# One shared inverse square root for two head norms, and an output projection whose first token block runs two outputs ahead of its second

## The chip, the core and the metric

The kernel runs on one NeuronCore of a Trainium2 chip. Five engines work side by side, each through its own queue in order: TensorE (PE, with its weight loads PEld), VectorE (DVE), ScalarE (ACT), GpSimd (POOL) and SyncE (SP, which only issues transfers). They meet at semaphores. The metric is device time in microseconds (us) of one execution; lower is better.

## The reference, cut to what matters

One layer of a recurrent decoder runs over 1104 token columns: 16 meta tokens, 8 sequences of 8 sample tokens and 1024 prompt tokens. Between two feed-forward halves stands the mixing part, and the change lies only there:

```python
z = h @ lp['w_in']
u_r, g_r, u_m, z_m, q_g, k_g, v_g, g_g, a_lr = jnp.split(z, _split_points(), axis=-1)
...
y_m = jax.nn.sigmoid(z_m) * (head_rmsnorm(hm, lp['ml_norm_g']) + lp['ml_skip'] * cm)   # mLSTM mixer, h = num / denom
y_g = head_rmsnorm(og, lp['gla_norm_g']) * jax.nn.silu(g_g)                            # GLA mixer
y = jnp.concatenate([y_r, y_m, y_g], axis=-1) @ lp['w_out']
...
def head_rmsnorm(h, g):                       # 4 heads of 96
    y = h * lax.rsqrt(jnp.mean(h * h, axis=-1, keepdims=True) + EPS)
    return y.reshape(Bsz, L, H * Dh) * g
```

Both mixers are recurrent over chunks of tokens: a chunk needs the state that the chunk before it left.

## The kernel before

**Stages.** The program does the first feed-forward half, the mixing part (`mix`, some 840 to 1345 us in the profile), the rest of `w_out` together with the start of the second feed-forward half, and that half. Every big product is three products of fp32r pieces (high by high, low by high, high by low), and a weight tile is split by ACT (`whi`) and DVE (`wlo`), both in the helper `split`, L115 and L116.

**Blocks and chunks.** The tokens stand in three blocks of 336, 384 and 384 columns, and in nine chunks of 128 (chunk 0 has 80, with the sample tokens), three to a block. In `mix`, PE does the input projections (`unit`, tile `pw`, line L210 of the helper `gemm3`), which write z to DRAM, and beside them both mixers chunk by chunk. `m1`, `m2`, `m3` are the mLSTM of a chunk (scores; state and outputs `num`; head norm, gate and the split into `ys`), `g1`, `g2`, `g3` the same of the GLA (output `o_`). `msamp` and `gsamp` do the sample sequences of chunk 0. The loop over `c` writes m1 and g1 of chunk c, then `fin` (m3 and g3) of chunk c-1, then m2 and g2 of chunk c. `fin` of chunk 0 comes at c = 4, since its samples come late. In `ylru`, the third mixer's output of a block is split into `ys[b]`.

**What sets the order.** The program isn't run in the order of the code. A list scheduler orders it before the run, with its own idea of durations: everything in `tc.high_priority` (the mixers) goes first where it is ready, and the projections and `w_out` fill in. The engines then run that fixed order.

**Buffers that matter here.** A tag of a pool has so many slots, and a new tile of it waits until one is free. `T4`/`TT` share the tag `t` (4 slots), `G4`/`GT` the tag `tg` (3 slots), `zg` (the gate inputs of m3 and of g3) has a single slot, and the split weights have 7. `ys[0]` takes the slot of the operands of block 0, so `ylru(0)` holds two `tg` tiles until the last input projection of block 0 has read them:

```python
if j == 1:
    ys[b] = slot(b)
if j == 2:
    ylru(b)
```

**The norm.** m3 and g3 each square (ACT), sum by head (DVE) and call `rsq` (L119 to L127): 2 integer instructions and 3 Newton steps of 3, all on DVE and each waiting for the one before, on tiles of 128 partitions by 4 heads. m3 also folds its denominator `dn` in. Then ACT scales the four heads, PE transposes (`to_f`, tile `pyT`, L982), and DVE and ACT finish `y` and split it into `ys`.

**w_out.** At c = 7 the products of blocks 0 and 1 with `w_out` are written (tile `pwo`): eight outputs d of 24 matmuls for each block, from two PSUM banks. Those of block 2 follow in `wout2` (L1662), after the broadcast of the next norm (`rbp`, L259).

Of the kernel before, what the change touches and what calls it, by code (L numbers as in the profile page):

```python
# [10 lines left out]
AF = mybir.ActivationFunctionType  # L11
OP = mybir.AluOpType
AX = mybir.AxisListType
# [6 lines left out]
EPS = 1e-6  # L20
# [29 lines left out]
def tile_step(ctx, tc, A, O):  # L50
    nc = tc.nc
    V, S, G, PE = nc.vector, nc.scalar, nc.gpsimd, nc.tensor
# [12 lines left out]
    def pa(name):  # L65
        return psum["a"].tile([128, 512], F32, tag="a", name=name)
# [37 lines left out]
    slots, ys = {}, {}  # L104
# [9 lines left out]
    def split(hi, lo, x):  # L114
        S.copy(hi, x)  # L115
        V.tensor_tensor(lo, x, hi.bitcast(F32), OP.subtract)  # L116

    def rsq(tp, v, p, n, tag=""):
        y = tp.tile([128, 8], F32, tag="rsy" + tag, name="rsy", bufs=RB)[:p, :n]  # L119
        a = tp.tile([128, 8], F32, tag="rsa" + tag, name="rsa", bufs=RB)[:p, :n]  # L120
        V.tensor_scalar(a.bitcast(I32), v.bitcast(I32), 1, None, OP.arith_shift_right)
        V.tensor_scalar(y.bitcast(I32), a.bitcast(I32), -1.0, float(0x5F3759DF), OP.mult, OP.add)
        for _ in range(3):
            V.tensor_tensor(a, y, y, OP.mult)
            V.scalar_tensor_tensor(a, a, -0.5, v, OP.mult, OP.mult)
            V.scalar_tensor_tensor(y, a, 1.5, y, OP.add, OP.mult)
        return y  # L127
# [56 lines left out]
    def wraw(pool):  # L184
        return pool.tile([128, 4, 256], F32, tag="raw", name="wraw", bufs=2)

    def wpair(pool):
        return [pool.tile([128, 4, 128], F32R, tag=tag, name=tag, bufs=7) for tag in ("whi", "wlo")]

    def wload(*parts):  # L190
        raw = wraw(P["wp"]).rearrange("p k f -> p (k f)").rearrange("p (k f) -> p k f", f=128)
        for c, w, src in parts:
            if src is None:
                G.memset(raw[:, :, c : c + w], 0.0)
            else:
                nc.sync.dma_start(raw[:, :, c : c + w], src)
        u = []
        for c in range(2):
            u.append(wpair(P["wp"]))
            split(*u[c], raw[:, 4 * c : 4 * c + 4, :])  # L200
        return [h for h, _ in u], [l for _, l in u]
# [4 lines left out]
    def gemm3(p, w, x, ks, wsl, xsl):  # L206
        i, tot = 0, 3 * len(ks)
        for ww, xx in ((w[0], x[0]), (w[0], x[1]), (w[1], x[0])):
            for k in ks:
                PE.matmul(p, wsl(ww, k), xsl(xx, k), start=i == 0, stop=i == tot - 1)  # L210
                i += 1
# [300 lines left out]

    wo = A["w_out"].rearrange("(k p) f -> p k f", p=128)

    def w_out(bs, out):
        for d in range(8):
            u = wload((0, 128, wo[:, :, d * 128 : d * 128 + 128]))
            for b in bs:
                n, t0 = NB[b], 16 if b == 0 else 0
                p = pa("pwo")  # L520
                gemm3(p[:, t0:n], u, ys[b], range(8), wblock, lambda x, k: x[:, k, t0:n])
                out(b, d, p[:, t0:n])


# [12 lines left out]
    def mix(  # L537
# [73 lines left out]
        mt = ph.enter_context(tc.tile_pool(name="mt", bufs=2, reuse_waits="tile"))  # L611

        def U(shape, tag, bufs=None, dt=F32):
            pool = me if tag in ("um", "gr", "cm", "sm", "vx", "num0", "o0", "qf0", "vt0", "qe0", "klT0", "vx0") else mt
            return pool.tile(shape, dt, tag=tag, name=tag, bufs=bufs)

        def TT(p=128, n=384):
            return U([128, 388], "t", 4)[:p, :n]

        def T4(e=96):  # L620
            return U([128, 388], "t", 4)[:, : 4 * e].rearrange("p (h e) -> p h e", h=4)

        def GT(p=128, n=384):
            return U([128, 388], "tg", 3)[:p, :n]

        def G4(e=96):
            return U([128, 388], "tg", 3)[:, : 4 * e].rearrange("p (h e) -> p h e", h=4)
# [311 lines left out]
            nc.scalar.dma_start(O["s_n"], nt)  # L939


        def m3(b, j, x):
            cm, o, m, num, et = x[:5]
            dn = U([128, 4], "dn")[:m]
            V.scalar_tensor_tensor(dn, num[:m, :, 96], -1.0, num[:m, :, 96], OP.mult, OP.max)
            V.tensor_tensor(dn, dn, et[:m, 32:36], OP.max)
            V.reciprocal(dn, dn)
            sq = T4()
            S.activation(sq[:m], num[:m, :, 0:96], AF.Square)
            ss = U([128, 4], "ssm")[:m]  # L950
            V.tensor_reduce(ss, sq[:m], AX.X, OP.add)
            V.tensor_tensor(ss, ss, dn, OP.mult)
            V.scalar_tensor_tensor(ss, ss, 1.0 / 96.0, dn, OP.mult, OP.mult)
            V.tensor_scalar(ss, ss, EPS, None, OP.add)
            rr = rsq(mt, ss, m, 4, "m")
            V.tensor_tensor(rr, rr, dn, OP.mult)
            hn = sq
            for h in range(4):
                S.mul(hn[:m, h, :], num[:m, h, 0:96], rr[:, h : h + 1])
            z = U([128, 3, 128], "zg", 1)  # L960
            nc.sync.dma_start(z[:, :, :m], zd["z"][:, :, OFF[b] + o : OFF[b] + o + m])
            y = TT().rearrange("p (k t) -> p k t", k=3)
            for k in range(3):
                S.mul(y[:, k, :m], cm[:, k, :m], skh[:, k : k + 1])
            p = to_f(pn2, hn, m)
            for k in range(3):
                V.scalar_tensor_tensor(y[:, k, :m], p[:, k, :m], ngh[:, k : k + 1], y[:, k, :m], OP.mult, OP.add)
            V.scalar_tensor_tensor(y[:, :, :m], z[:, :, :m], 1.0, y[:, :, :m], OP.add, OP.mult)
            split(ys[b][0][:, 2:5, o : o + m], ys[b][1][:, 2:5, o : o + m], y[:, :, :m])
            if b == 2 and j == 2:  # L970
                nc.sync.dma_start(O["p_C"].rearrange("h d e -> d h e"), c1[:, :, 0:96])
                pn = pn2("pn")
                PE.transpose(pn[:4, 0:96], c1[:, :, 96], ident[:96, :96])
                nt = U([32, 128], "cst")
                S.copy(nt[:4, :96], pn[:4, 0:96])
                nc.scalar.dma_start(O["p_n"], nt[:4, :96])

        def to_f(pool, src, m):
            p = pool("pyT").rearrange("p (k t) -> p k t", k=4)
            s = src.rearrange("p h e -> p (h e)")  # L980
            for k in range(3):
                PE.transpose(p[:, k, :m], s[:m, k * 128 : k * 128 + 128], ident[:m, :m])  # L982
            return p
# [264 lines left out]
                    nc.sync.dma_start(O["s_S"][:, 2 * a + i].rearrange("s k v -> k s v"), ssm[64 * i : 64 * i + 48])  # L1248


        def g3(b, j, x):
            to, m, o_ = x[:3]
            sq = G4()
            S.activation(sq[:m], o_[:m], AF.Square)
            ss = U([128, 4], "ssg")[:m]
            V.tensor_reduce(ss, sq[:m], AX.X, OP.add)
            V.tensor_scalar(ss, ss, 1.0 / 96.0, EPS, OP.mult, OP.add)
            rr = rsq(mt, ss, m, 4, "g")
            on = sq
            for h in range(4):  # L1260
                S.mul(on[:m, h, :], o_[:m, h, :], rr[:, h : h + 1])
            g = U([128, 3, 128], "zg", 1)
            nc.sync.dma_start(g[:, :, :m], zd["g"][:, :, to : to + m])
            p = to_f(pg2, on, m)
            y = GT().rearrange("p (k t) -> p k t", k=3)
            V.tensor_tensor(y[:, :, :m], g[:, :, :m], p[:, 0:3, :m], OP.mult)
            o = to - OFF[b]
            split(ys[b][0][:, 5:8, o : o + m], ys[b][1][:, 5:8, o : o + m], y[:, :, :m])
            if b == 2 and j == 2:
                for a in range(2):  # L1270
                    for i in range(2):
                        nc.sync.dma_start(O["p_S"][2 * a + i], s1[64 * i : 64 * i + 48, a, i, :])
# [32 lines left out]
        el8 = U([128, 2, 8], "el8", 1)  # L1305

        def fin(x):
            m3(*x[0])
            g3(*x[1])

        x, x0 = None, None
        preps = {
# [2 lines left out]
        for c in range(9):  # L1315
            with tc.high_priority(offset=BOOST):
                b, j = divmod(c, 3)
                for f, i in preps.get(c, ()):
                    f(i)
                xm, xg = m1(b, j), g1(b, j)  # L1320
# [11 lines left out]
                x = (b, j, m2(b, j, xm)), (b, j, g2(b, j, xg))  # L1332
                if c == 0:
                    x0, x = x, None
# [4 lines left out]
        with tc.high_priority(offset=BOOST):  # L1339
            fin(x)  # L1340
# [138 lines left out]
    with ExitStack() as ph:  # L1479
# [84 lines left out]
        c0, n = THIRDS1[0][1], THIRDS1[0][0]  # L1564
# [25 lines left out]
        for b, (n, c0) in enumerate(THIRDS1):  # L1590
            x = xq.tile([128, 8, 384], F32, tag="xo", name="xo", bufs=2)[:, :, :n]
# [29 lines left out]
    with ExitStack() as ph:  # L1621
# [94 lines left out]
        for j, (n, c0, chunks, s0) in enumerate(THIRDS2):  # L1716
            x = tp.tile([128, 8, 384], F32, tag="xo", name="xo", bufs=2)[:, :, :n]
# [9 lines left out]
            ss = tp.tile([128, 3, 3], F32, tag="ssf", name="ssf", bufs=2)  # L1727
# [14 lines left out]
            for i, (o, m) in enumerate(chunks):  # L1742
                dst = O["y_sample"] if s0 + o < 0 else O["y_prompt"][s0 + o : s0 + o + 128, :]
                for q in range(2):
                    h = slice(q * 512, q * 512 + 512)
# [60 lines left out]
```

## Time and profile before

| what | value |
|---|---|
| three runs | 2164.37, 2165.81, 2166.42 us; median 2165.81 us |
| the profiled execution | 2165.65 us, of which the span of the page is 2163.9 us |
| PE busy | 2089.4 us, 97% of the span |
| DVE busy | 1299.5 us, 60% |
| ACT busy | 914.1 us, 42% |

Shares are averages over stages with different limits, so a change of one stage is read in that stage. A busy PE is not PE at its peak, since matmuls overlap: two that follow each other start closer together than one lasts. A product of plain fp32 operands stands twice in the trace and once in the program's order.

### The profile page before, as it was taken

The numbers are of one execution on the slowest core, as the hardware profiler recorded it, in microseconds if no ns is written. First come the engines' busy times: TensorE is split into PE (matmuls) and PEld (weight loads), VectorE is DVE, ScalarE is ACT, GpSimd is POOL, SyncE is SP. The second block draws the span as 40 slices with busy tenths as digits, with TensorE's granted clock in tenths as the row PEclk, the third lists the DMA queues.
The fourth block names the chain that finished last, engine by engine and source line by source line (L and its number), as shares of the span: only waits on it lengthen the run. The fifth ranks groups of instructions, "written<-read, shape, count | busy, mean of one in ns | idle before, by whom it ended". The sixth has DMA issues, their size and how long they took to land.

```text
span 2163.9 us, 38185 instructions
## 1 busy us (share of the span) xinstructions
PE 2089.4 (97%) x14600; PEld 2040.0 (94%) x14600; DVE 1299.5 (60%) x2861; ACT 914.1 (42%) x1965; POOL 270.7 (13%) x284
## 2 busy tenths in 40 slices
PE   6999999999999999999999899999999999999997
PEld 6999999999989999978997789999999999998997
DVE  7765555663565545866777786776555566356342
ACT  5433232342443434635655673443233234254332
POOL 0222232211100011000000000022323221000000
PEclk8999999999999999999999899999999999999999
DMA  6322222235574544444434245522322224667342
GB/s 213 105 83 95 90 71 70 82 126 167 187 245 138 200 138 116 131 139 129 114 87 111 75 119 156 190 69 82 99 83 81 70 81 133 201 222 244 127 142 83
DMA packets 292555, 275.50 MB, mean 127 GB/s; under 512 B 46751, under 2 KB 277188, under 8 KB 291860
## 3 DMA queue, kind: packets, MB, share of 16 engines
q1 hardware_dynamic: 287580, 271.27, 40.0%
q10 hardware_dynamic: 4792, 1.78, 0.4%
q8 instruction: 115, 1.88, 0.4%
q14 instruction: 68, 0.56, 0.1%
HBM read 212.99 MB, written 60.01 MB: 126 GB/s over the span
## 4 chain that ended last, share of the span: by engine, by line
PE 86%; DVE 5%; DMA 4%; ACT 3%; issue 1%; SPq 0%; POOL 0%; DVEq 0%; ACTq 0%; POOLq 0%
PE p L503 22%; PE b L365 15%; PE c L365 10%; PE a L365 10%; PE pw L210 9%; PE a L411 4%; PE b L411 4%; PE pwo L210 3%; DMA wraw<-in_ffn_w_dram 1%; PE pq L837 1%; PE pA L1039 1%; PE pwo L1662 1%; DVE wlo L116 1%; DMA hr<-hidden 1%; DMA bcc<-z_bc 0%
## 5 line engine op out<-in xcount | busy, mean ns | idle before, releaser
L116 DVE TENSOR_TENSOR wlo<-wraw,whi 128x512 fp32r<-128x512 f32 x508 | 360.7, 728 | 338.9 <-ACT whi L115 228.9
L115 ACT CAST whi<-wraw 128x512 fp32r<-128x512 f32 x508 | 302.7, 618 | 576.8 <-PE p L503 157.0
L503 PE MATMUL p<-h,whi 128*128 128x384 f32 (+2 forms) x2080 | 402.2, 331 | 0.7 <-ACT whi L115 0.6
L503 PEld LDWEIGHTS p<-h,whi 128*128 128x128 f32 x2080 | 354.9, 189 | 1.7 <-ACT whi L115 1.4
L365 PE MATMUL b<-op,whi 128*128 128x256 f32 (+2 forms) x1728 | 255.9, 289 | 0.4 <-DVE c L372 0.4
L365 PEld LDWEIGHTS b<-op,whi 128*128 128x128 f32 x1728 | 233.6, 189 | 0.7 <-DVE c L372 0.7
L503 PE MATMUL p<-h,wlo 128*128 128x384 f32 (+2 forms) x1040 | 222.3, 331 | 0.0
L372 DVE TENSOR_TENSOR c<-p,b 128x256 f32<-128x256 f32 (+2 forms) x216 | 94.6, 439 | 175.1 <-PE b L365 162.1
L342 POOL TENSOR_TENSOR ws<-wraw 128x512 f32<-128x512 f32 x72 | 105.2, 1461 | 728.0 <-DMA wraw<-in_ffn_w_dram 473.4
L503 PEld LDWEIGHTS p<-h,wlo 128*128 128x128 f32 x1040 | 181.0, 190 | 0.0
L365 PE MATMUL c<-op,whi 128*128 128x256 f32 (+2 forms) x1152 | 172.8, 289 | 0.3 <-DVE op L116 0.3
L365 PE MATMUL a<-op,whi 128*128 128x256 f32 (+2 forms) x1152 | 172.5, 289 | 0.0
L365 PEld LDWEIGHTS c<-op,whi 128*128 128x128 f32 x1152 | 155.7, 189 | 0.5 <-DVE op L116 0.5
L365 PEld LDWEIGHTS a<-op,whi 128*128 128x128 f32 x1152 | 155.1, 189 | 0.0
L365 PE MATMUL b<-op,wlo 128*128 128x256 f32 (+2 forms) x864 | 144.4, 289 | 0.0
L115 ACT CAST whi<-ws 128x512 fp32r<-128x512 f32 x144 | 88.4, 618 | 132.4 <-PE b L365 79.4
L365 PEld LDWEIGHTS b<-op,wlo 128*128 128x128 f32 x864 | 122.6, 189 | 0.0
L116 DVE TENSOR_TENSOR wlo<-ws,whi 128x512 fp32r<-128x512 f32 x144 | 100.2, 696 | 2.2 <-PE b L411 1.7
L210 PE MATMUL pw<-sh,whi 128*128 128x384 f32 (+1 forms) x480 | 97.3, 339 | 1.6 <-DVE stg L581 1.6
L372 DVE TENSOR_TENSOR c<-c 128x256 f32<-128x256 f32 (+2 forms) x144 | 62.8, 436 | 59.2 <-PE c L365 58.9
L210 PE MATMUL pw<-sh,wlo 128*128 128x384 f32 (+1 forms) x480 | 98.0, 339 | 0.0
L365 PE MATMUL a<-op,wlo 128*128 128x256 f32 (+2 forms) x576 | 96.4, 289 | 0.5 <-DVE wlo L116 0.5
(466 smaller groups left out, 3382.0 us busy)
## 6 DMA issues: line engine op xcount, KB each, us to landing
wraw<-in_ffn_w_dram SPq DMA_DIRECT2D x224, 512.0 KB
hr<-hidden SPq DMA_DIRECT2D x88, 192.0 KB
hidden<-h SPq DMA_DIRECT2D x36, 256.0 KB
wraw<-in_w_in_dram SPq DMA_DIRECT2D x16, 512.0 KB
wraw<-in_w_out_dram SPq DMA_DIRECT2D x16, 512.0 KB
wraw<-in_ffn_w_dram SPq DMA_DIRECT2D x24, 256.0 KB
hidden<-h SPq DMA_DIRECT2D x18, 296.0 KB
hidden<-h SPq DMA_DIRECT2D x18, 288.0 KB
```

The source lines that it names most:

```text
L115: S.copy(hi, x)
L116: V.tensor_tensor(lo, x, hi.bitcast(F32), OP.subtract)
L210: PE.matmul(p, wsl(ww, k), xsl(xx, k), start=i == 0, stop=i == tot - 1)
L342: G.tensor_tensor(t, x, y, op)
L365: PE.matmul(t[:, :n], ww[:, k, :], xx[:, k, :], start=first and i == 0, stop=i == 11, skip_group_check=True,)
L372: V.tensor_tensor(out, x, t[:, :n], OP.add)
L411: PE.matmul(p, w[:, k, :], x[:, k, :], start=c == 0, stop=c == 23)
L503: PE.matmul(ps_[e], t[k // 2][a][:, k % 2, e * 128 : e * 128 + 128], hs[k0 + k][b], start=k0 == 0 and i == 0, stop=k0 + nk == NFB and i == ...
L837: PE.matmul(p[:96, h, :m], wt[:, kb, sl, 0:96], cm[:, kb, :m], start=i == 0, stop=i == len(ks) - 1)
L1039: PE.matmul(p[:, a], x[:, a], y[:, a], start=True, stop=True)
L1662: PE.matmul(p, u[k // 4][a][:, k % 4, :], ys[2][b][:, k, :], start=i == 0, stop=i == 23)
```

## The change

`m3` and `g3` no longer have an `rsq` each: a new `norm` squares and sums both mixers' heads into one tile of 8 columns and calls `rsq` once. `w_out` writes block 0's output d, and block 1's output d - 2 behind it, so that up to three outputs' weights are held.

```diff
     def w_out(bs, out):
-        for d in range(8):
-            u = wload((0, 128, wo[:, :, d * 128 : d * 128 + 128]))
-            for b in bs:
+        u = {}
+        for i in range(10):
+            for b, d in ((bs[0], i), (bs[1], i - 2)):
+                if not 0 <= d < 8:
+                    continue
+                if d not in u:
+                    u[d] = wload((0, 128, wo[:, :, d * 128 : d * 128 + 128]))
                 n, t0 = NB[b], 16 if b == 0 else 0
                 p = pa("pwo")
-                gemm3(p[:, t0:n], u, ys[b], range(8), wblock, lambda x, k: x[:, k, t0:n])
+                gemm3(p[:, t0:n], u[d], ys[b], range(8), wblock, lambda x, k: x[:, k, t0:n])
                 out(b, d, p[:, t0:n])
...
-        def m3(b, j, x):
-            cm, o, m, num, et = x[:5]
+        def norm(xm, xg):
+            m, num, et, o_ = xm[2], xm[3], xm[4], xg[2]
             dn = U([128, 4], "dn")[:m]
...
-            sq = T4()
-            S.activation(sq[:m], num[:m, :, 0:96], AF.Square)
-            ss = U([128, 4], "ssm")[:m]
-            V.tensor_reduce(ss, sq[:m], AX.X, OP.add)
-            V.tensor_tensor(ss, ss, dn, OP.mult)
-            V.scalar_tensor_tensor(ss, ss, 1.0 / 96.0, dn, OP.mult, OP.mult)
-            V.tensor_scalar(ss, ss, EPS, None, OP.add)
-            rr = rsq(mt, ss, m, 4, "m")
-            V.tensor_tensor(rr, rr, dn, OP.mult)
-            hn = sq
+            ss = U([128, 8], "ssm")[:m]
+            sm, sg_ = T4(), G4()
+            for i, (sq, x) in enumerate(((sm, num[:m, :, 0:96]), (sg_, o_[:m]))):
+                S.activation(sq[:m], x, AF.Square)
+                V.tensor_reduce(ss[:, 4 * i : 4 * i + 4], sq[:m], AX.X, OP.add)
+            for _ in range(2):
+                V.tensor_tensor(ss[:, 0:4], ss[:, 0:4], dn, OP.mult)
+            V.tensor_scalar(ss, ss, 1.0 / 96.0, EPS, OP.mult, OP.add)
+            rr = rsq(mt, ss, m, 8, "m")
+            V.tensor_tensor(rr[:, 0:4], rr[:, 0:4], dn, OP.mult)
+            return rr, sm, sg_
...
-        def g3(b, j, x):
+        def g3(b, j, x, rr, on):
             to, m, o_ = x[:3]
-            sq = G4()
-            S.activation(sq[:m], o_[:m], AF.Square)
-            ss = U([128, 4], "ssg")[:m]
-            V.tensor_reduce(ss, sq[:m], AX.X, OP.add)
-            V.tensor_scalar(ss, ss, 1.0 / 96.0, EPS, OP.mult, OP.add)
-            rr = rsq(mt, ss, m, 4, "g")
-            on = sq
             for h in range(4):
-                S.mul(on[:m, h, :], o_[:m, h, :], rr[:, h : h + 1])
+                S.mul(on[:m, h, :], o_[:m, h, :], rr[:, 4 + h : 5 + h])
...
         def fin(x):
-            m3(*x[0])
-            g3(*x[1])
+            rr, sm, sg_ = norm(x[0][2], x[1][2])
+            m3(*x[0], rr, sm)
+            g3(*x[1], rr, sg_)
```

**What moves on PE at the first chunk's norm.** In PE's queue of before, in the middle of the input projections (`pw`), stand the transposes of chunk 1's mLSTM output (`pyT<-ident,t`), and soon after them chunk 2's state product (`pI<-c_9306,qf`):

```order
L1021 MATMUL pv<-ident,vf 128x128 x3
L921 MATMUL pI<-sm,qx 80x97 x2
L982 MATMUL pyT<-ident,t 128x128 x3
L210 MATMUL pw<-sh_7291,whi 128x384 x2
...
L1039 MATMUL pA<-qbd_9301,qk 32x2 x2
L875 MATMUL pI<-c_9306,qf 128x97 x4
L210 MATMUL pw<-sh_8865,whi 128x384 x8
```

In PE's queue of the change the same transposes and the same state product (lines L992 and L880 there) stand behind the last input projection:

```order
L210 MATMUL pw<-sh_8865,wlo 128x384 x8
L210 MATMUL pwo<-sh_11897,whi 128x320 x2
L1179 MATMUL pkl<-ident,h 128x128 x2
L1242 MATMUL pO<-sm,qx 80x96 x8
L992 MATMUL pyT<-ident,tg 128x128 x3
L210 MATMUL pwo<-sh_11897,whi 128x320 x2
L992 MATMUL pyT<-ident,t 128x128 x3
L1031 MATMUL pv<-ident,vf 128x128 x3
L1242 MATMUL pO<-sm,qx 80x96 x8
L880 MATMUL pI<-c_9306,qf 128x97 x4
```

What moved is chunk 1's finish and, behind it, the mLSTM of chunks 2 and 3: the first row shown there is the last of the input projections.

**On DVE at that norm.** In DVE's queue of the change, `ylru(0)`'s two splits (`sl_11898<-tg`) stand directly ahead of the sum of the GLA's squares (`ssm<-tg`) and of the joint `rsq`:

```order
L116 TENSOR_TENSOR sl_11898<-tg,sh_11897 128x336 x2
L1139 TENSOR_TENSOR h<-qk,h 128x128
L957 TENSOR_REDUCE ssm<-tg 128x4
L1074 COPY_PREDICATED at_9300<-lev_6806,pA 128x64x4
L1176 TENSOR_TENSOR h<-h,qk 128x256
L960 TENSOR_SCALAR ssm<-ssm 128x8
```

Before, chunk 1's mLSTM sum (`ssm<-t`) went on to its own `rsq` without waiting for a `tg` tile. Now both halves wait for those splits.

**At the end of the mixing part.** The tail of DVE's queue of the change: chunk 8's gate product of the GLA (`tg<-zg,pyT`) stands in the middle of the `rsq` of the next norm, whose result builds `dg` for the broadcast `rbp`:

```order
L978 SCALAR_TENSOR_TENSOR t<-zg,t 128x384
L241 MEMSET rsv 128x5
...
L121 TENSOR_SCALAR rsa<-rsv 128x5
...
L124 TENSOR_TENSOR rsa<-rsy 128x5
L1269 TENSOR_TENSOR tg<-zg,pyT 128x384
L125 SCALAR_TENSOR_TENSOR rsa<-rsa,rsv 128x5
...
L126 SCALAR_TENSOR_TENSOR rsy<-rsa,rsy 128x5
L258 TENSOR_SCALAR dg<-ident,rsy 128x128 x2
```

Before, chunk 8 was finished earlier, and that `rsq` stood by itself behind the last products of `w_out`.

## Rows read from the trace of the kernel before

**Rows 1.** The page's chain that ended last, share of the span by engine.

```profile
PE 86%; DVE 5%; DMA 4%; ACT 3%; issue 1%; SPq 0%; POOL 0%; DVEq 0%; ACTq 0%; POOLq 0%
```

**Rows 2.** Busy time and granted clock by stretch.

```profile
core 0: us, PE busy (x) PEld busy (x) DVE busy (x) ACT busy (x) POOL busy (x), PEclk, DMA share, GB/s
1030.00:1146.00 116.00, 116.00 (x841) 107.73 (x840) 84.51 (x280) 62.98 (x192) 6.18 (x14) 1.00 0.40 103
1175.60:1260.60 85.00, 68.41 (x456) 61.35 (x454) 65.49 (x278) 57.19 (x190) 3.46 (x9) 0.86 0.30 74
1253.00:1331.40 78.40, 78.12 (x562) 75.98 (x561) 62.33 (x237) 48.70 (x146) 1.18 (x3) 0.98 0.45 130
1190.00:1200.00 10.00, 7.91 (x34) 7.24 (x35) 7.07 (x35) 7.29 (x26) 0.00 (x0) 0.54 0.29 70
```

**Rows 3.** Timeline of DVE: ylru(0)'s splits; the key scaling of chunks 5 and 8.

```profile
1145.98 0.91 DVE L116 TENSOR_TENSOR sl<-tg,sh 128x336 fp32r<-128x336 f32 x2
...
1175.59 0.54 DVE L855 TENSOR_TENSOR kT<-kT,wk 128x384 f32<-128x384 f32 x1
...
1260.59 0.55 DVE L855 TENSOR_TENSOR kT<-kT,wk 128x384 f32<-128x384 f32 x1
```

**Rows 4.** Timeline of PE: one chunk's mLSTM products, and later chunks' first.

```profile
1167.53 1.55 PE L837 MATMUL pq<-cmc,wkS 128*96 128x128 f32 x12 [0.87 <-DMA cmc<-z_cm]
...
1170.23 1.03 PE L875 MATMUL pI<-c,qf 96*128 96x97 f32 x8
1171.19 0.86 PE L1245 MATMUL pc<-vx,klT 80*64 80x384 f32 x2
...
1172.73 0.50 PE L843 MATMUL pkT<-ident,qf 96*128 96x96 f32 x4
...
1174.08 0.86 PE L1245 MATMUL pc<-vx,klT 80*64 80x384 f32 x2
...
1177.36 0.86 PE L884 MATMUL pc<-v,kT 128*96 128x97 f32 x8
1178.07 0.64 PE L1039 MATMUL pA<-h 128*128 128x128 f32 x4
...
1195.59 2.82 PE L837 MATMUL pq<-cmc,wkS 128*96 128x128 f32 x12
...
1218.94 2.88 PE L837 MATMUL pq<-cmc,wkS 128*96 128x128 f32 x12 [1.29 <-DMA cmc<-z_cm]
...
1253.03 2.77 PE L837 MATMUL pq<-cmc,wkS 128*96 128x128 f32 x12
```

**Rows 5.** Groups of DVE by line and form, 1146 to 1332 us: rsq.

```profile
L126 DVE SCALAR_TENSOR_TENSOR rsy<-rsa,rsy 128x4 f32<-128x4 f32 x42 | 6.5, 161 | 0.6
L124 DVE TENSOR_TENSOR rsa<-rsy 128x4 f32<-128x4 f32 x42 | 6.5, 161 | 0.5
L122 DVE TENSOR_SCALAR rsy<-rsa 128x4 int32<-128x4 int32 x14 | 2.4, 170 | 0.2
```

**Rows 6.** Timeline of DVE: the gate slot zg read by g3, then by m3.

```profile
1202.58 0.39 DVE L1266 TENSOR_TENSOR tg<-zg,pyT 128x240 f32<-128x240 f32 x1
...
1206.04 0.56 DVE L968 SCALAR_TENSOR_TENSOR t<-zg,t 128x384 f32<-128x384 f32 x1 [0.74 <-DMA zg<-z_z]
```

**Rows 7.** Timelines of PE and DVE at the end of the mixing part.

```profile
1325.28 0.27 PE L982 MATMUL pyT<-ident,t 128*128 128x128 f32 x1
...
1343.74 0.61 PE L1291 MATMUL ssp<-ones,sqo 128*128 128x1 f32 x4 [0.63 <-ACT sqo L1288]
1347.69 2.76 PE L259 MATMUL rbp<-dg,ones 128*128 128x128 f32 x10 [3.34 <-DVE dg L258]
1350.64 2.93 PE L1662 MATMUL pwo<-sh,whi 128*128 128x384 f32 x8 [0.19 <-ACT rb L262]
...
1325.89 0.86 DVE L967 SCALAR_TENSOR_TENSOR t<-pyT,pc,t 128x128 f32<-128x128 f32 x3
...
1347.25 0.83 DVE L258 TENSOR_SCALAR dg<-ident,rsy 128x128 f32<-128x128 f32 x4
```

More of the change, by code (lines that the diff above doesn't have):

```diff
@@ L947, in m3 @@
             V.reciprocal(dn, dn)
-            sq = T4()
-            S.activation(sq[:m], num[:m, :, 0:96], AF.Square)
-            ss = U([128, 4], "ssm")[:m]
-            V.tensor_reduce(ss, sq[:m], AX.X, OP.add)
-            V.tensor_tensor(ss, ss, dn, OP.mult)
-            V.scalar_tensor_tensor(ss, ss, 1.0 / 96.0, dn, OP.mult, OP.mult)
-            V.tensor_scalar(ss, ss, EPS, None, OP.add)
-            rr = rsq(mt, ss, m, 4, "m")
-            V.tensor_tensor(rr, rr, dn, OP.mult)
-            hn = sq
+            ss = U([128, 8], "ssm")[:m]
[9 more added lines that the diff above has]
+            return rr, sm, sg_
+        def m3(b, j, x, rr, hn):
+            cm, o, m, num, et = x[:5]
             for h in range(4):
```

## The prediction

> **What bounds the kernel now.** I read the chain that ended last first [rows 1]: 86% of it is PE, so work that leaves another engine is worth time only where PE waits for that engine. The table by stretch [rows 2] says where that is, inside the part that the change touches. From 1030 to 1146 us PE is busy in every one of the 116.00 us. From 1253.0 to 1331.4 it is again full, 78.12 of 78.40. Between them, from chunk 5's key scaling on DVE at 1175.59 to chunk 8's at 1260.59 [rows 3], PE is busy in 68.41 of 85.00 us and its granted clock is 0.86. That is the starved stretch: projections are done, `w_out` has few products ready, and PE waits for the chain of the mixers, which runs mostly on DVE (65.49 of 85.00 busy). A chunk starts there with its `pq` group, and the shortest cycle seen is 1195.59 to 1218.94, 23.35 us [rows 4].
>
> **Part 1, the joint norm.** Per chunk, two inverse square roots of 2 + 9 instructions become one, and one more small instruction goes: 12 fewer for nine chunks, 108 in all. One takes 161 to 170 ns [rows 5], and I take a tile of 8 columns at the price of one of 4. 108 x 0.161 = 17.4 us of DVE time. Before 1146 us and after 1253 us PE is full, so there it is worth nothing: the cover is projections ahead and `w_out` behind. In the starved stretch about four chunks are finished, 4 x 12 x 0.161 = 7.7 us. That would be the gain if nothing moved.
>
> **Part 2, what moves.** The joint norm needs a `tg` tile for the GLA's squares as well, and takes one sum only when both exist. For chunk 1 the third `tg` slot comes free only behind `ylru(0)`'s splits, which wait for block 0's last projection. So in the order of the change, chunk 1's finish, chunk 2's state product and chunk 3's mLSTM stand behind the projections. They were filler inside them. Counted in the two orders, one chunk's `pq`, `pkT`, `pS` and `pk` (5.2 us), two chunks' `pI`, `pN`, `pc` and `pD` (5.7), and transposes, `klT` and `pA` products (about 4.2) leave the projections: together 15.1 us of PE time, estimated from issue distances such as 12 `pq` products in 1.55 us, 8 `pI` in 1.03 and 8 `pc` in 0.86 [rows 4]. PE being full there, `ylru(0)`'s split comes 15 us earlier: it ends at about 1146.4 (0.91 us in two from 1145.98 [rows 3]), then at about 1131.3.
>
> Then the starved stretch is longer, for those products and their DVE work now lie in it. From `ylru(0)`'s split to chunk 8's key scaling the order of the change has 425 DVE instructions, before 348. Each at the mean of its own kind in the trace, the 425 sum to 140.0 us. At the same measure the 278 from [rows 3]'s second to its third row sum to 81.3 us, more than their busy time because neighbours overlap, and they took 85.0 us: 0.956 us of durations per us. 140.0 / 0.956 = 146.4 us, so chunk 8's key scaling comes at 1131.3 + 146.4 = 1277.7. Its `pq` stood 1260.59 - 1253.03 = 7.6 us ahead [rows 3, 4]; now 1270.1, 17 us later than before.
>
> **Part 3, two outputs ahead.** `w_out` has 384 products for the first two blocks. Before, block 1's products of an output follow block 0's, so block 0 stops with them until `ys[1]` is there; 58 products stood between the last projection and chunk 8's `pq`, 246 from there to chunk 8's last transposes at about 1327.5 (those of the mLSTM begin at 1324.8 and are followed 2.3 us later by the GLA's; the last row of them shown is at 1325.28 [rows 7]), and 80 behind. With two ahead, 145 stand before chunk 8's `pq`, 239 up to the transposes and none behind. The mixers' own products in that last part fall from 162 to 121, for the later chunks' scores are done sooner. 74.5 us, PE full, becomes about 66.0: 8.5 less, for 7 x 0.17 is 1.2 and 41 mixer products of 0.1 to 0.2 are the rest. PE must also wait some 2 us for chunk 8's norm, since no `w_out` is left to cover it. The last transposes then come at 1270.1 + 66.0 + 2 = 1338.1.
>
> **Part 4, the tail.** Before, chunk 8 was done under the 80 products left, and behind the last of them came `ssp` at 1343.74, the next norm, `rbp` at 1347.69 and the first product of `wout2` at 1350.64 [rows 7]. Now chunk 8's finish stands last. From its transposes: `y` of m3 (three in 0.86 us [rows 7]) and the gate, about 2.4; then `zg`, a single slot, is freed and loaded again, 3.1 us from its last reader's end to its next reader (1202.97 to 1206.04 [rows 6]); the product with the gate 0.55; what is left of the next `rsq`, 1.5; then `dg`, `rbp` and the first product, with small joins, about 2.5. Together 10.0 us, so 1348.1, against 1350.64: **-2.5 us**.
>
> Against that stands the same slot inside the stretch. In the order of the change the m3 and g3 reads of `zg` come closer together: at the durations of DVE's instructions between them 2.3, 0.6, 3.0, 1.0, 2.0, 2.7, 2.6, 0.6 and 2.1 us, where the reload needs 3.1. Before, it already cost 0.74 us once [rows 6]. If every shortfall in the starved cycles stalled the chain it were +4.6, if other work covered it 0; a good part is covered, since DVE is idle for a fifth of the time there anyway, and I take +1.4. Sum: -2.5 + 1.4 = **-1.1 us**. The profiled execution took 2165.65 us, 0.16 below the median of the three runs, so no correction: **2164.5 us**. A measurement of this kernel tells about 0.2% (4.3 us) from no change, and this is inside it.
>
> **The rivals.** *A, near tie* as above: the DVE saving, the earlier fill by `w_out` and the shorter last part pay for the longer starved stretch. Each term may miss by a few us: 2158.5 to 2170.
>
> *B, a clear gain.* For it speaks that DVE now has 12 short dependent instructions less in each chain: these are where it idles between neighbours. If DVE runs the 140.0 us without gaps, chunk 8 comes 6.4 us sooner; if the reloads of `zg` are hidden in the stretch and in the tail, 1.4 and 3.1 more. Together -10.9, 2153.6. Against it: DVE never ran a starved stretch in this trace without gaps.
>
> *C, slower.* One mechanism: between chunks 3 and 4, 4 and 5, and 6 and 7 the order of the change has no `w_out` product at all, only 52, 52 and 70 mixer products, and DVE durations of 18.4, 16.0 and 19.8 us. If such a cycle is bound not by the sum of DVE's work but by the chain of one chunk through PE, ACT and DVE (state product, outputs, norm, transposes, next state product), which the joint norm lengthens by making the mLSTM wait for the GLA, each lasts the 23.35 us of [rows 4], not the 18.9 that my sum has for it: 3 x 4.45 = +13.4, so 2177.9. It decides from about 20.8 us per cycle on (+5.7, so 2170.2, just beyond the bound). For it speaks that the cycle of 23.35 us had DVE free for a fifth of it.
>
> *D, the clock.* In 1190 to 1200 us, where PE was busy in 7.91 of 10.00 us, its granted clock was 0.54 [rows 2], so mostly 1.2 GHz, and the `pq` group there took 2.82 us against 1.55 at 2.4 GHz [rows 4]. If the three unfilled cycles ran wholly at 1.2 GHz, some 175 products of 0.12 us would cost double on the path, +21 at most, and +17 with what waits hide: 2181.5. The Trainium skill has a rule that speaks for it ("TensorE: Matmul & The Clock Gate", section "What's actually happening"): the throttled clock is the array's resting state, and activity is what releases it. This trace agrees in direction, 0.54 in those thin 10 us and 1.00 where PE is full; by that rule a change that thins PE out pays D, by my sum only what 0.86 already holds.
>
> **How the numbers follow.** Chances: A 0.46, B 0.28, C 0.20, D 0.06. The likeliest is A, so 2164.5; its own range is 2158.5 to 2170. The range of 2152 to 2177 takes in B with the DVE bound wholly used, and C up to just below its full price; left out are C's upper half, and D. Faster by over 0.2%: B and a quarter of A, its lower end, 0.40. Same: 0.29. Slower: C, D and A's upper edge, 0.31.
>
> **What would show it.** `ylru(0)`'s split near 1131 us, not 1146; chunk 8's `pq` near 1270 and its last transposes near 1338; `wout2` from about 1348. The three unfilled cycles at 18 to 20 us, with DVE the releaser; at 23 us and with DVE half idle, C is right. A granted clock below 0.75 between 1135 and 1270 would be D. Idle time of DVE put down to `zg` over 5 us in the stretch breaks the +1.4. The prediction is wrong as a whole if chunk 1's finish does not stand behind the projections, or if split weights, three outputs of which are now held, make PE wait for `whi` or `wlo` in the last part.

## The result and the profile after

The change is slower: 2185.79 us median of five runs (2181.67 to 2187.81) against 2165.81 (2162.57 to 2168.82), ratio 1.0092, 95% interval [1.0079, 1.0105], about +20 us. The forecast was a near tie at 2164.5 us with a range up to 2177. The profiled execution took 2187.81 us.

The page of the kernel after: span, busy time of PE, and the chain that ended last by engine, to be read against [rows 1].

```profile
span 2186.1 us, 38095 instructions
...
PE 2093.8 (96%) x14600; PEld 2044.0 (94%) x14600; DVE 1294.4 (59%) x2753; ACT 915.2 (42%) x1965; POOL 269.9 (12%) x284
...
PE 82%; DMA 6%; DVE 6%; ACT 3%; issue 2%; SPq 1%; POOL 0%; DVEq 0%; ACTq 0%; POOLq 0%
```

DVE has 108 instructions fewer (2861 before), so the saving was made. PE is busy 4.4 us longer and idle 17.8 us longer; together they are the 22.2 us of the span. Where that lies, the table by stretch of the kernel after tells: the input projections end at 1140.30 us, `w_out`'s products start to flow at about 1204, chunk 8's `pq` starts at 1291.7, and `rbp` ends the mixing part at 1366.7.

```profile
core 0: us, PE busy (x) PEld busy (x) DVE busy (x) ACT busy (x) POOL busy (x), PEclk, DMA share, GB/s
1140.30:1204.50 64.20, 52.61 (x348) 46.00 (x347) 47.44 (x174) 41.02 (x134) 2.09 (x6) 0.81 0.34 84
1204.50:1291.70 87.20, 71.91 (x508) 68.41 (x508) 60.35 (x207) 54.63 (x177) 2.86 (x8) 0.90 0.30 78
1291.70:1358.00 66.30, 63.34 (x453) 62.85 (x451) 41.34 (x128) 33.51 (x89) 0.41 (x1) 1.00 0.53 161
...
1140.30:1366.70 226.40, 190.06 (x1313) 178.31 (x1311) 154.45 (x531) 132.01 (x406) 5.35 (x15) 0.89 0.38 104
```

The same stretch of the kernel before, from its last input projection to its `rbp`:

```profile
1162.80:1347.70 184.90, 163.47 (x1125) 152.21 (x1124) 139.33 (x533) 113.50 (x352) 5.37 (x12) 0.94 0.42 117
```

So the projections end 22.5 us sooner and `rbp` comes 19.0 us later. PE is busy 26.6 us more there and idle for 36.3 us instead of 21.4. Of the 26.6 us, 22.5 are what left the projections, since PE was full there; the 4.1 left over go with the lower granted clock (0.89 instead of 0.94), at which products last longer (the 100 `pA` products of 128x128 take 315 ns on average, before 291).

The timeline of DVE in the kernel after, for [rows 3]: `ylru(0)`'s splits, and the key scaling of chunks 3, 4, 5 and 8.

```profile
1129.17 0.93 DVE L116 TENSOR_TENSOR sl<-tg,sh 128x336 fp32r<-128x336 f32 x2
...
1166.62 0.56 DVE L860 TENSOR_TENSOR kT<-kT,wk 128x384 f32<-128x384 f32 x1
...
1190.80 0.56 DVE L860 TENSOR_TENSOR kT<-kT,wk 128x384 f32<-128x384 f32 x1
...
1205.59 0.55 DVE L860 TENSOR_TENSOR kT<-kT,wk 128x384 f32<-128x384 f32 x1
...
1297.54 0.56 DVE L860 TENSOR_TENSOR kT<-kT,wk 128x384 f32<-128x384 f32 x1 [0.64 <-ACT kT L849]
```

The timeline of PE in the kernel after, for [rows 4, 7]: the `pq` groups of chunks 5 to 8, and the end of the mixing part.

```profile
1197.69 1.73 PE L842 MATMUL pq<-cmc,wkS 128*96 128x128 f32 x12 [2.44 <-DMA cmc<-z_cm]
...
1232.36 2.24 PE L842 MATMUL pq<-cmc,wkS 128*96 128x128 f32 x12 [2.87 <-DMA cmc<-z_cm]
...
1259.18 2.84 PE L842 MATMUL pq<-cmc,wkS 128*96 128x128 f32 x12 [6.05 <-DMA cmc<-z_cm]
...
1291.72 1.47 PE L842 MATMUL pq<-cmc,wkS 128*96 128x128 f32 x12
...
1358.05 0.86 PE L992 MATMUL pyT<-ident,tg 128*128 128x128 f32 x3 [2.12 <-ACT tg L1264]
1359.11 1.00 PE L992 MATMUL pyT<-ident,t 128*128 128x128 f32 x3 [0.20 <-ACT t L969]
...
1366.69 2.96 PE L259 MATMUL rbp<-dg,ones 128*128 128x128 f32 x10 [5.29 <-DVE dg L258]
1369.85 2.93 PE L1666 MATMUL pwo<-sh,whi 128*128 128x384 f32 x8 [0.20 <-ACT rb L262]
```

The split comes about where it was forecast (it ends at 1130.1 us, forecast 1131.3), the stretch from chunk 8's `pq` to the last transposes takes 67.4 us (forecast 68.0), and the tail from there to `wout2` 10.7 us (forecast 10.0). The one stretch that misses is from the split to chunk 8's key scaling: 1297.54 instead of 1277.7.

What it hides is seen in the transposes of one chunk, `t` for the mLSTM and `tg` for the GLA. Chunk 3 in the kernel before:

```profile
1163.81 0.55 PE L982 MATMUL pyT<-ident,t 128*128 128x128 f32 x3
...
1217.17 0.49 PE L982 MATMUL pyT<-ident,tg 128*128 128x128 f32 x3
```

The same in the kernel after:

```profile
1208.87 0.27 PE L992 MATMUL pyT<-ident,tg 128*128 128x128 f32 x1
...
1210.38 0.27 PE L992 MATMUL pyT<-ident,t 128*128 128x128 f32 x1
```

Before, the mLSTM was **53 us ahead** of the GLA at chunk 3, and the lead shrank chunk by chunk to 2 us at chunk 8 (1324.8 against 1327.0). After, both finish together, at the GLA's time: at chunk 3 the GLA is 8 us earlier, the mLSTM 46.6 us later. This lead is what the prediction did not look for. The mLSTM's five cycles from there to chunk 8 take 148.7 us, before 161.0, so chunk 8 comes 34.3 us late: not because its cycles became longer, but because they begin late.

The wait is carried from one chunk to a later one by `cmc`, which has two slots. A chunk's scores `pq` read it first and its finish in m3 reads it last, so the load for a new chunk waits for the finish of an earlier one. These are the load for chunk 3 and the first `pq` behind it, in the kernel before and then in the kernel after:

```profile
1102.59 0.53 SPq L804 DMA_DIRECT2D cmc<-z_cm  x1
1108.32 1.47 PE L837 MATMUL pq<-cmc,wkS 128*96 128x128 f32 x12
...
1157.43 0.53 SPq L809 DMA_DIRECT2D cmc<-z_cm  x1
1160.26 2.87 PE L842 MATMUL pq<-cmc,wkS 128*96 128x128 f32 x12
```

In the kernel after this load is also PE's longest wait between 1140 and 1292 us, 11.4 us in three waits; before it was 2.2 us in two (1162 to 1253 us). What a third slot would give was not run.

### The profile page after: what moved, and what is told of

Read it like the earlier page. It is cut to its first block, busy times and chain, and to the rows that moved or that the text cites. A ratio compares the mean times of both kernels' runs of the same rounds, so it can differ in the third digit from the quotient of the medians.

```text
span 2186.1 us, 38095 instructions
## 1 busy us (share of the span) xinstructions
PE 2093.8 (96%) x14600; PEld 2044.0 (94%) x14600; DVE 1294.4 (59%) x2753; ACT 915.2 (42%) x1965; POOL 269.9 (12%) x284
## 4 chain that ended last, share of the span: by engine, by line
PE 82%; DMA 6%; DVE 6%; ACT 3%; issue 2%; SPq 1%; POOL 0%; DVEq 0%; ACTq 0%; POOLq 0%
PE p L503 19%; PE b L365 15%; PE c L365 10%; PE a L365 10%; PE pw L210 9%; PE b L411 4%; PE a L411 4%; PE pwo L210 3%; DMA wraw<-in_ffn_w_dram 2%; PE pq L842 1%; PE pA L1049 1%; DVE wlo L116 1%; DVE op L116 1%; ACT whi L115 1%; PE pwo L1666 1%
```

## Experiments

Theories on record were **move** (products left the projections' cover at chunk 1), **coupling** (every joint norm lengthens a cycle), **order** (`w_out` two ahead costs), and after the first four runs **lead** (a joint norm holds the mixer that is ahead until the other has come). The table gives each run's ratio to runs of before on the same chip, what that makes of 2165.8 us (as a difference from before), and from its trace the start of the mLSTM's transposes of chunk 8 and of `rbp`.

| run | ratio [95%] | us | chunk 8 | `rbp` |
|---|---|---|---|---|
| before | 1 | 0 | 1324.8 | 1347.7 |
| the change | 1.0092 [1.0079, 1.0105] | +20 | 1359.1 | 1366.7 |
| e1_norm_only | 1.0076 [1.0051, 1.0101] | +16 | 1357.1 | 1364.6 |
| e2_wout_only | 0.9982 [0.9966, 0.9999] | -4 | 1324.5 | 1345.6 |
| e4b_block0_apart | 1.0106 [1.0086, 1.0127] | +23 | 1368.8 | 1376.4 |
| e5_move_alone | 1.0074 [1.0056, 1.0093] | +16 | 1355.7 | 1365.8 |
| e9_joint_from5 | 1.0073 [1.0059, 1.0087] | +16 | 1357.1 | 1364.7 |
| e9_joint_from7 | 0.9995 [0.9980, 1.0010] | -1 | 1336.1 | 1347.3 |
| e3b_sqo12 | 1.0108 [1.0092, 1.0123] | +23 | 1363.8 | 1371.5 |
| e8b_wout_sqo | 0.9976 [0.9967, 0.9985] | -5 | 1319.3 | 1343.4 |
| e10_newton1 | 0.9962 [0.9950, 0.9975] | -8 | 1312.8 | 1336.4 |
| e12_skew | 1.0089 [1.0068, 1.0111] | +19 | 1337.8 | 1364.6 |
| e13_gla_on_pool | 0.9995 [0.9985, 1.0005] | -1 | 1327.9 | 1347.7 |
| e14_sqo_newton1 | 0.9944 [0.9930, 0.9958] | -12 | 1317.0 | 1336.3 |

**The two parts apart.** e1_norm_only is the change with `w_out` as before, e2_wout_only is before with the new `w_out`; each takes the one half of the diff that stands ahead.

> Joint norm alone, w_out in its old order. Three theories. Move: the products of chunks 1 to 3 that left the cover of the projections cost the time; then +18 to +26 us against before, with the last input projection near 1140 us. Coupling: the joint norm ties the two mixers' chains in every starved cycle; then the same +18 to +26. Order: the new order of w_out costs the time; then 0 to +5. If w_out two outputs ahead is a gain, as forecast, this kernel is slower than the whole change by 3 to 6.

> The order of w_out alone, both norms separate. Order: +15 to +22 us against before. Move and coupling: -6 to +1, since chunk 1 stays inside the projections (the last of them near 1163 us) and block 0's products fill more of the starved stretch (78 instead of 58 before chunk 8's scores).

The order of `w_out` is a small gain by itself, its interval just clear of 1; the joint norm alone is slower. The order theory is out. That the new order helps beside the joint norm by 3 to 6 us, as expected, is not seen: whether it helps or hurts there is not told apart (1.0076 and 1.0092, intervals overlap).

**Move or coupling.** e4b_block0_apart keeps the first chunks apart; `m3x` and `g3x` are m3 and g3 of before:

```diff
         def fin(x):
+            if x[0][0] == 0:
+                m3x(*x[0])
+                g3x(*x[1])
+                return
             rr, sm, sg_ = norm(x[0][2], x[1][2])
```

> The whole change, but chunks 0 to 2 keep two separate norms, so that chunk 1's finish and the mLSTM of chunks 2 and 3 stay inside the projections; chunks 3 to 8 have the joint norm. Move: -6 to +3 us against before. Coupling: +10 to +20, as six of the nine joint norms remain, all of those in the starved stretch.

e5_move_alone makes chunk 1's mLSTM wait for a `tg` slot, in the kernel before:

```diff
-            sq = T4()
+            sq = G4() if (b, j) == (0, 1) else T4()
```

> The kernel before with two norms and the old w_out, but the tile for the squares of chunk 1's mLSTM is taken from the slots of tg, so that its finish waits for ylru(0) as in the change. Move: +14 to +22 us against before, projections ending near 1140 us. Coupling: -2 to +5, as no norm is joint.

Each is slow without the other: +23 with nothing moved out of the projections at chunk 1, beyond what either theory expected, and +16 without a joint norm, as move expected and where coupling had no more than +5. So neither theory is the whole. What the two have in common is that the mLSTM has lost its lead: in e5_move_alone chunk 3's transposes of the mLSTM begin at 1207.1 us and in e4b_block0_apart at 1216.7, where before had 1163.8. In e5_move_alone the GLA's chunk 8 also comes late, at 1347.6 us instead of 1327.0; whether by the slot that it has to share or by the late mLSTM is not told apart.

**Where the lead is lost.** The condition of `fin` in e4b_block0_apart becomes `if 3 * x[0][0] + x[0][1] < 5` (and `< 7`):

> New order of w_out, separate norms up to chunk 4, joint norms from chunk 5 on. In the trace of before the mLSTM's transposes of chunk 3 run some 50 us ahead of the GLA's, those of chunk 5 some 28 us, those of chunk 7 some 14 us. Lead: a joint norm from chunk k on costs the lead that the mLSTM has at k, since both then go at the GLA's pace; 28 of 50 us here, so about half of what the kernel with joint norms from chunk 3 lost: +4 to +12 us against before. Coupling of each cycle at an equal price: four of six norms, +12 to +17. Move: -6 to +2, for nothing leaves the projections.

> The same with joint norms for chunks 7 and 8 alone. Lead: 14 of 50 us are left at chunk 7, and PE is full there with w_out: -4 to +4 us against before. Coupling at an equal price: two of six, +4 to +8. Move: -6 to +2.

With joint norms from chunk 5 on nothing differs from e2_wout_only until chunk 5. The timeline of PE, chunk 5's transposes, chunk 8's first one and `rbp`, in e2_wout_only:

```profile
1238.21 0.68 PE L986 MATMUL pyT<-ident,t 128*128 128x128 f32 x3
...
1261.53 0.49 PE L986 MATMUL pyT<-ident,tg 128*128 128x128 f32 x3
...
1324.48 0.27 PE L986 MATMUL pyT<-ident,t 128*128 128x128 f32 x1
...
1345.56 2.96 PE L259 MATMUL rbp<-dg,ones 128*128 128x128 f32 x10 [3.34 <-DVE dg L258]
```

and in e9_joint_from5:

```profile
1261.39 0.42 PE L1036 MATMUL pyT<-ident,tg 128*128 128x128 f32 x1
...
1262.88 0.85 PE L1036 MATMUL pyT<-ident,t 128*128 128x128 f32 x3
...
1357.11 1.00 PE L1036 MATMUL pyT<-ident,t 128*128 128x128 f32 x3
...
1364.66 2.96 PE L259 MATMUL rbp<-dg,ones 128*128 128x128 f32 x10 [5.26 <-DVE dg L258]
```

The GLA of chunk 5 comes at the same time to 0.2 us; the mLSTM comes 24.7 us later, just behind it. The stretch in which it waits, 1230 to 1260 us, by the table of e2_wout_only:

```profile
1230.00:1260.00 30.00, 23.06 (x171) 20.69 (x172) 26.79 (x120) 24.63 (x81) 1.91 (x4) 0.95 0.34 92
```

and of e9_joint_from5:

```profile
1230.00:1260.00 30.00, 21.26 (x123) 18.44 (x123) 20.57 (x76) 18.53 (x59) 0.75 (x2) 0.73 0.26 68
```

DVE falls from 26.79 to 20.57 us busy, and PE's granted clock from 0.95 to 0.73: with one mixer alone there is less to do beside its waits. Chunk 8 then comes 32.6 us later, and `rbp` 19.1. So 8 us were added behind chunk 5: the mLSTM's cycles from there on are 31.4 us on average, against 28.8 in e2_wout_only, which the lead alone does not explain. From the last input projection to `rbp`, these two kernels have the same PE products. First e2_wout_only, then e9_joint_from5:

```profile
1167.80:1345.60 177.80, 157.24 (x1126) 147.47 (x1124) 139.02 (x534) 113.88 (x352) 4.79 (x12) 0.94 0.43 121
1166.60:1364.70 198.10, 166.49 (x1126) 153.92 (x1124) 137.25 (x486) 114.88 (x352) 4.66 (x12) 0.89 0.40 110
```

Of the 20.3 us more, PE is idle for 11.0 and busy for 9.3, at a lower granted clock (0.89 instead of 0.94): the durations of the same products sum to 348.0 us instead of 337.8. From chunk 7 on, the lead lost is 9.8 us (1295.0 to 1304.9), chunk 8 comes 11.6 later, and `rbp` only 1.7.

My dose was wrong: I expected half the loss for half the lead, and +16 us lies in the range that coupling had (+12 to +17); its equal price per cycle fails at chunk 7, where it had +4 to +8 and -1 was measured. The difference between the two columns explains the table better: in all of e1, e3b, e4b, e5, e9_joint_from5 and the change `rbp` is 13 to 15 us less late than chunk 8, against before (for e3b, e4b and e9_joint_from5, which have the new `w_out`, against e2_wout_only). That is about what the products of `w_out` that used to stand behind chunk 8 cover: 80 of them in the kernel before, some 13.6 us at 0.17 us each. A delay of chunk 8 up to that is free within the noise, as in e9_joint_from7; in the other runs about all beyond it is paid. For the change: 34.3 us late, less 15.3, is the 19.0 us by which `rbp` is late.

**Is it the slot?** e3b_sqo12 gives the GLA's tiles of chunks 1 and 2 another buffer:

```diff
-            sm, sg_ = T4(), G4()
+            sm = T4()
+            sg_ = U([128, 384], "sqo", 1).rearrange("p (h e) -> p h e", h=4) if c1 else G4()
...
-            y = GT().rearrange("p (k t) -> p k t", k=3)
+            y = (on.rearrange("p h e -> p (h e)") if (b, j) in ((0, 1), (0, 2)) else GT()).rearrange("p (k t) -> p k t", k=3)
```

> The whole change, but for chunks 1 and 2 the squares and the output of the GLA use the idle buffer of w_out's squares (sqo), so that their joint norm waits for no tg slot. Slot: the wait for the third tg slot is the whole cause, then 0 to +4 us against before. Lead: with the joint norm the mLSTM still has to wait for the GLA of chunk 2, which ends behind the projections; only chunk 1's finish and chunk 2's state come back under them: +8 to +18.

+23 us, more than either theory expected: without the slot's wait the joint norm is as slow, so that slot is not needed for the loss. Chunk 1's mLSTM finishes under the projections again (1090.0 us), but chunk 2's waits for the GLA of chunk 2 and comes at 1170.9. The same buffers with separate norms, and the new `w_out`:

> Separate norms, the new order of w_out, and the GLA's tiles of chunks 1 and 2 in sqo instead of a tg slot. Lead: the mLSTM keeps its lead, and the GLA may finish chunks 1 and 2 sooner; if w_out's block 0 opens before 1195 us: -10 to -3 us against before. If the GLA's pace is set by something else than the slot, the same as the order of w_out alone: -5 to 0.

A small gain, -5 us, not distinguishable from e2_wout_only's -4.

**The DVE saving without the tie.** In e10_newton1 the loop of `rsq` runs once for the head norms, so the norms are coarser:

```diff
-        for _ in range(3):
+        for _ in range(steps):
...
-            rr = rsq(mt, ss, m, 4, "m")
+            rr = rsq(mt, ss, m, 4, "m", 1)
```

> The kernel before, with one Newton step instead of three in the two head norms: it leaves out part of the inverse square root, so that DVE has 12 small instructions fewer per chunk, as many as the joint norm takes away, and no mixer has to wait for the other. If that DVE work is worth what the first part of the prediction says when nothing moves, about 7.7 us: -9 to -4 us against before. If DVE's time is not what PE waits for: -2 to +2.

-8 us, [-0.50%, -0.25%]: the same 12 instructions per chunk are worth about the 7.7 us of part 1, if nobody has to wait for them.

**A skewed pairing.** In e12_skew, `fin` keeps the GLA of a chunk for one turn:

```diff
+            c = 3 * x[0][0] + x[0][1]
+            if c < 5:
+                m3x(*x[0])
+                if c < 4:
+                    g3x(*x[1])
+            else:
+                rr, sm, sg_ = norm(x[0][2], held[0][2])
+                m3(*x[0], rr, sm)
+                g3(*held[0], rr, sg_)
+                if c == 8:
+                    g3x(*x[1])
+            held[:] = [x[1]]
```

> New order of w_out; separate norms up to chunk 4, and from chunk 5 on a joint norm of a chunk's mLSTM with the GLA of the chunk before, the last GLA by itself. Lead: in the trace of w_out's order alone the GLA's transposes of chunks 4 to 7 come at 1244.9, 1261.5, 1280.9 and 1305.5 us, the mLSTM's of chunks 5 to 8 at 1238.2, 1263.0, 1295.0 and 1324.5, so the mLSTM hardly waits, and the GLA at most 19 us, which about its slack covers: -6 to +4 us against before, where the joint norm of the same chunk from 5 on cost 16. Coupling: any joint norm lengthens a chunk's cycle; then +10 to +16 here too.

A miss: +19 us, where lead had at most +4. The mLSTM of chunk 5 is 9.8 us late (1248.0), somewhat more than the 6.7 us that the expectation's own times give, and chunk 8's comes only 13 us late. But now the GLA is tied to the mLSTM. PE's timeline of e12_skew, the GLA's transposes of chunk 7, the mLSTM's of chunk 8, the GLA's of chunk 8:

```profile
1336.90 0.27 PE L1036 MATMUL pyT<-ident,tg 128*128 128x128 f32 x1
...
1337.85 0.31 PE L1036 MATMUL pyT<-ident,t 128*128 128x128 f32 x1
...
1357.99 1.01 PE L1036 MATMUL pyT<-ident,tg 128*128 128x128 f32 x3 [1.45 <-ACT tg L1331]
```

and on its DVE, for the GLA of chunk 7:

```profile
1352.03 0.56 DVE L1313 TENSOR_TENSOR tg<-zg,pyT 128x384 f32<-128x384 f32 x1 [7.77 <-DMA zg<-z_g]
```

The GLA of chunk 7 comes 31 us later than in e2_wout_only, that of chunk 8 29.9 us, beyond any cover, and on the way to chunk 8's DVE waits 7.77 us for the single `zg` slot. The mLSTM's cycles from chunk 5 to 8 (1248.0, 1276.3, 1307.2, 1337.8) are 29.9 us on average, against 28.8 in e2_wout_only: the tie lengthens a cycle by 1.1 us and above all shifts whoever was ahead. That speaks for lead as the larger part, with its slack sized wrongly, and leaves some coupling (here 3.5 us in three cycles, 8 in e9_joint_from5).

**Two versions beside it.**

> The kernel e8b_wout_sqo with the nine Newton instructions of the GLA's inverse square root moved from DVE to GpSimd (as twelve simpler ones): DVE loses 9 small instructions per chunk, and no mixer waits for the other. If DVE's time in the starved stretch is what counts: -11 to -6 us against before, that is 2 to 6 better than e8b_wout_sqo. If the GLA's own chain counts and GpSimd takes longer for each: e8b_wout_sqo's -5 is lost, 0 to +8.

Only the engine of the GLA's Newton steps, and their number (twelve instead of nine), differ from e8b_wout_sqo, and most of its gain is gone. Lines of GpSimd in e13_gla_on_pool, 1146 to 1332 us, grouped:

```profile
L125 POOL TENSOR_TENSOR rsa<-rsa,ssg 128x4 f32<-128x4 f32 x21 | 6.1, 291 | 1.6
L127 POOL TENSOR_TENSOR rsy<-rsy,rsa 128x4 f32<-128x4 f32 x21 | 5.3, 252 | 1.8
L126 POOL TENSOR_SCALAR rsa<-rsa 128x4 f32<-128x4 f32 x21 | 5.1, 245 | 1.7
L124 POOL TENSOR_TENSOR rsa<-rsy 128x4 f32<-128x4 f32 x21 | 4.7, 225 | 98.2 <-DVE rsy L122 82.4 <-DVE rsa L137 14.8
```

Four instructions of 225 to 291 ns make 1.01 us per step, where DVE's three take 0.48 [rows 5]: the chain is longer, though DVE is freer. That the longer chain is what took the gain is argued, not shown.

> The kernel e8b_wout_sqo with one Newton step instead of three in the two head norms, which leaves out part of the inverse square root: 12 small DVE instructions fewer per chunk with separate norms and the new order of w_out. If the two gains add (-8 and -5): -15 to -10 us against before, and about 30 less than the change, with as many DVE instructions as it has. If both gains come out of the same idle time: -9 to -6.

-12 us: the gains add. This version, with the coarser norm, beats both kernels; it has as many DVE instructions as the change (2753) and is 1.5% faster. With the norm unchanged the best is e8b_wout_sqo, -5 us.

## Why the prediction was wrong, step by step

- **Part 1** held: 12 instructions fewer per chunk, an 8-column tile at 163 to 170 ns for most, and 207 for one, against 161 to 170; worth 8 us where it costs no wait (e10_newton1).
- **Part 2, what moves** held in place: the split begins 16.8 us earlier (forecast 15). In all 22.5 us of PE work left the projections and not 15.1.
- **The step that failed** is "140.0 / 0.956 = 146.4 us". It took DVE's pace from the stretch of before in which the two mixers were independent, one up to 50 us ahead, and put at nothing that the joint norm takes this lead away. Measured: 1297.54 - 1129.17 = 168.4 us. The durations of those DVE instructions in the trace of the change sum to 144.1 us, so the sum was short by 4 us, and the pace was 0.86 instead of 0.956, which is the rest. Up to chunk 5's key scaling it was 0.91, in the three cycles behind it, two of which hold `w_out` products, 0.81. DVE's time was not what set the pace.
- **Part 3** held: 67.4 us instead of 68.0. **Part 4** held: 10.7 instead of 10.0. The sum had the lost cover in it, with chunk 8's finish standing last ("none behind"). For the same reason nothing was left to hide the late chunk 8.
- **The zg term** (+1.4): DVE waits for `zg` 4.8 us in the starved stretch of after and 4.7 in that of before, so next to nothing. The slot that did cost PE a wait is `cmc`, which the prediction does not price.

**Rival C** was right in its mechanism, the mLSTM made to wait for the GLA, and wrong in its place and price: the three unfilled cycles, `pq` to `pq`, took 22.3, 15.1 and 26.8 us, 7.5 more than my 3 x 18.9; the rest of the loss is in filled cycles. What decides is less how long such a cycle is than that the mLSTM's last five cycles begin 46.6 us later. **Rival B** is out: its DVE bound without gaps is the contrary of what happened. **Rival D** is a part, and follows from the waits: the granted clock is 0.81 between the last projection and the first `w_out` products, and 0.86 from 1135 to 1270 us, where D was to show below 0.75. PE is busy 4.1 us longer than what moved explains, a fifth of the loss, and 9.3 of 20.3 us in e9_joint_from5 against e2_wout_only, where nothing moved; no run holds the clock still, so its own price stays open. The Trainium skill ("TensorE: Matmul & The Clock Gate", section "What's actually happening") has the throttled clock as the resting state, released by activity. The rows agree in direction: 0.95 to 0.73 in e9_joint_from5's 30 us where PE's busy time fell.

Shown by runs: the joint norm is what costs (e1, e2); it costs without the slot and without the move (e3b, e4b); losing the lead by other means costs about as much (e5); where the mLSTM comes no more than 9.8 us later at the first joint norm, it is free within the noise (e9_joint_from7); the DVE work is worth 8 us (e10). Open: why the mLSTM's cycle stays near 30 us with either kernel, how much a tie lengthens it where no lead is lost, and what more `cmc` slots would change.

## What to carry to other kernels

Before joining two chains' small work into one instruction, compare when each chain arrives there, chunk by chunk: the one that runs ahead waits for the other from then on, and the lead it had under other work's cover is gone. A pace measured with two independent chains is no rate of the engine, and did not carry over here to chains in step (0.956 and 0.86). Look for the buffers with few slots that pass a late finish on to a later chunk. Count the filler that stands behind the last chunk: here a delay was free up to about that, and paid beyond.

## What was not expected of the hardware

In e13_gla_on_pool a GpSimd instruction on 128x4 takes 225 to 291 ns, 1.4 to 1.8 times DVE's 161 [rows 5]. Three steps are then 3.0 us of chain instead of 1.4, longer by 1.6 us, and free 1.4 us of DVE.
